# Inputs kept for the last pass: stored as one part and split anew, and two groups to a half of the tokens at a pass's turn

## The chip, the cores and the metric

The kernel runs on 1 core of one Trainium2 chip. The metric is the device time in microseconds: 1502.4 us is the median of 3 runs of the kernel before (1499.89 to 1511.44). One more execution was profiled; it took 1505.07 us.

## The reference

One decoder layer on x (2048 tokens, 1024 channels, float32). The projection is the part that the change touches:

```
hn = rms_norm(x, w_norm)
proj = hn @ w_in                      # 1024 -> 4104 columns
q_a, k_a, v_a, z_a, b_a, a_a, q_b, k_b, v_b, z_b = split(proj)
qkv = silu(causal_conv(q_a, k_a, v_a))        # 4 taps
o_a = gated_delta_rule(l2(q_a), l2(k_a), v_a, g(a_a), sigmoid(b_a))   # 4 heads, in chunks
o_a = rms_norm(o_a) * silu(z_a)
o_b = (softmax(q1 k1) - lam softmax(q2 k2)) v_b                       # 4 heads, causal
o_b = rms_norm(o_b) * silu(z_b)
out = x + concat(o_a, o_b) @ w_out
```

## The kernel before, in words

**Numbers.** Each float32 operand of a large matmul is split into a high part (rounded for the fast matmul format) and a low part (the remainder); a product is three matmuls, high by high, high by low and low by high. So the normalised, transposed input of 512 tokens (an *instance*) is a pair of tiles hh and hl, 128x8x512 each, 2 MB each; the weights of a group of 256 columns are a pair wh and wl, made from wr.

**Passes and groups.** The projection has three passes over halves of 1024 tokens (line 368): the first makes z_a and the six groups of q_a, k_a, v_a for the first half of the tokens (8 groups), the second makes all 16 groups for the second half, the third the attention's columns for the first half (8 groups). Each pass has two instances, so six in all: 0 and 1 in the first pass, 2 and 3 in the second, 4 and 5 in the third. Only two pairs hh, hl and two pairs wh, wl have room. A job is 24 matmuls with 512 moving columns or 48 with 256; a group has 4 jobs or more, half on its pass's first instance and half on its second.

**Inputs.** `x_load` (line 435) loads x in 16 tiles of 128 tokens, into two buffers xt and three buffers x5; `x_scale` normalises a tile (squares on ScalarE, a power on GpSimd, the scaling on VectorE), `x_split` (502) transposes it on TensorE into a PSUM tile tp and splits it: ScalarE copies tp to hh, VectorE subtracts hh from tp into hl. Instances 0 and 1 are needed again in the third pass as 4 and 5. `hx_store` (533) writes their hh and hl to DRAM in quarters while the first pass runs, and `hx_load` (546) reads them into the buffers that instances 2 and 3 leave.

**Weights.** `w_stream` (389) loads one group ahead into two buffers wr (one for each half of the 1024 rows), and splits a group once the group two places before it is through (`w_done`). The load of the next group waits for that split, since it needs wr.

**Order of jobs.** `in_jobs` (562) lists the jobs group by group. The last two groups of a pass are taken together: both on the first instance, then both on the second, so that the first instance is free earlier.

**What sets the order of everything.** The program has streams (generators), each of which yields its next step with an engine and a time. `Flow` (line 31) keeps modelled clocks of the engines and takes the step that could start first (`run`, line 207), and issues it; so the order of each engine's queue is fixed when the program is built, and an engine takes its queue strictly in that order. One changed step moves the ones around it on every engine. TensorE's queue mixes projection jobs with the delta rule's matmuls (tiles psg: a block of `gdn_a` is six matmuls with qk_h and qk_a; fsX makes its decays; then the scan over 16 chunks, with vh, o, S, rr), the transposes tp of x, and in the last third the attention. The loads and most stores go through SyncE's queue (SP).

**Names.** psi: PSUM tile of a projection job. za_s, zb_s, gdx, qk, v: DRAM stages for what the projection made. raw, acc: SBUF tiles of its epilogue. AL: lower triangles of the delta rule.

Of the kernel before, what the change touches and what calls it, by code (L numbers as in the profile page):

```python
# [8 lines left out]
F32 = mybir.dt.float32  # L9
F32R = mybir.dt.float32r  # L10
BF16 = mybir.dt.bfloat16
AF = mybir.ActivationFunctionType
ALU = mybir.AluOpType
# [4 lines left out]
P = 128  # L18
S = 2048
D = 1024  # L20
KT = D // P
# [8 lines left out]
TB = 512  # L30
# [3 lines left out]
class Flow:  # L34
# [119 lines left out]
    def dma(self, out, in_, run=1024, by="SP", **kw):  # L154

        if by == "SP":
            if len(self.dmas) > 7:
                self.free["SP"] = max(self.free["SP"], self.dmas[-8])
            self.op("SP", 475)
        else:  # L160
            self.op(by, 60)
            self.end += 415
        s = max(self.free["DMA"], self.end + 650)
        self.free["DMA"] = s + 4 * math.prod(out.shape) / 250 * (2 if run < 512 else 1)
        (self.nc.sync if by == "SP" else self.nc.scalar).dma_start(out=out, in_=in_, **kw)  # L165
        if by == "SP":
            self.dmas.append(self.free["DMA"] + 1200)
        return self.free["DMA"] + 1200
# [63 lines left out]
def hybrid_kernel(ctx: ExitStack, tc: tile.TileContext, x, w_norm, w_in, conv_w, a_log, dt_bias,  # L232
# [4 lines left out]
    out = out[0]  # L237
# [4 lines left out]
    dram = ctx.enter_context(tc.tile_pool(name="dram", bufs=1, space=DRAM))  # L242

    def r(ap):
        return ap.bitcast(F32R)

    def f(ap):
        return ap.bitcast(F32)
# [9 lines left out]
    zb_s = [dram.tile([P, S], F32, name=f"zb_s{h}") for h in range(H)]  # L258
    o_s = dram.tile([P, 2 * H, S], F32, name="o_s")
    part = dram.tile([S, D], F32, name="part")  # L260
    hx_s = [[dram.tile([P, KT, TB], F32, name=f"hx{i}_{j}") for j in range(2)] for i in range(2)]

    fl = Flow(nc)
    mm, tr, dma = fl.mm, fl.tr, fl.dma
# [118 lines left out]
    HX = {}  # L383
# [51 lines left out]
    def x_load():  # L435
        for n in range(16):

            def best():

                b = x_buf + ([(t_5[0], "ga")] if live5[0] < NX5 else [])  # L440
                return min(b) if b else None

            yield "SP", (lambda: best()[0]), best
            bf = best()
            if bf[1] == "wk":
                x_buf.remove(bf)
                xt = wk.tile([P, D], F32, name="xt", bufs=NXB)
            else:
                live5[0] += 1
                xt = ga.tile([P, D], F32, name="x5", bufs=NX5)  # L450
            n_xl[0] += 1
            t_x = []
            for hs in ([slice(0, TB), slice(TB, D)] if n == 0 else [slice(0, D)]):
                t_x.append(dma(out=xt[:, hs], in_=x[n * P:(n + 1) * P, hs]))
            xq[n] = (xt, t_x[0], bf[1])
            if n == 0:
                for i in range(2):
                    wnb.append(wk.tile([P, TB], F32, name="wnb", tag=f"t1_{i}"))
                    t_wn.append(dma(out=wnb[i], in_=bcast(w_norm)[:, i * TB:(i + 1) * TB]))
                dma(out=ident, in_=c_ident)  # L460
# [72 lines left out]
    def hx_store():  # L533

        for i in range(2):
            yield "SP", (lambda: max(x_ready[i].values())), lambda: all((i, t) in x_done for t in range(4))
            for kh in range(2):
                for j in range(2):
                    yield "SP", NOW, lambda: w_done[0] >= HXW + 3 * (4 * i + 2 * kh + j) // 4
                    t_hx[i] = dma(out=hx_s[i][j][:, kh * 4:kh * 4 + 4], in_=f(HX[i][j][:, kh * 4:kh * 4 + 4]))  # L540

    t_hx = [0.0] * 2
    HXW = 2
# [2 lines left out]
    def hx_load():  # L546
        for i in range(2):
            yield "SP", (lambda: max(t_xu[i + 2], t_hx[i])), lambda: x_used[i + 2]
            hx = (hn.tile([P, KT, TB], F32, name="hh"), hn.tile([P, KT, TB], F32, name="hl"))
            HX[i + 4] = tuple(r(h[:, :, :]) for h in hx)  # L550
            for kh in range(2):
                for j in range(2):
                    yield "SP", NOW, None
                    t = dma(out=hx[j][:, kh * 4:kh * 4 + 4], in_=hx_s[i][j][:, kh * 4:kh * 4 + 4])
                if kh == 0:
                    x_ready[i + 4] = {n: t for n in range(4)}
                x_late[i + 4] = t
            x_done.update((i + 4, n) for n in range(4))

    epi = []  # L560
# [1 line left out]
    def in_jobs():  # L562

        jobs = []
        for gi, (ip, half, kind, arg) in enumerate(groups):
            for tb in range(2):
                if kind == GA and (arg == 0 or gi == 0):
                    js = [[t] for t in range(4)]
                elif kind in (GA, GQ, GV):
                    js = [[2 * t, 2 * t + 1] for t in range(2)]  # L570
                else:
                    js = [c for c in range(2)]
                jobs += [(gi, tb, what) for what in js]
        last = [gi for gi in range(len(groups) - 1) if groups[gi + 1][0] != groups[gi][0]] if SWAP else []
        return sorted(jobs, key=lambda a: (a[0], 0) if a[0] not in last and a[0] + 1 not in last else
                      (a[0] + (a[0] + 1 in last) - 1, a[1]))

    SWAP = True

    def in_proj():  # L580
        KS = 2
# [1169 lines left out]
```

## Time and profile before

| | |
|---|---|
| median of 3 runs | 1502.4 us (1499.89 to 1511.44) |
| the profiled execution | 1505.07 us, span 1503.3 us from the first to the last instruction |
| busy: TensorE (PE), VectorE (DVE), ScalarE (ACT), GpSimd (POOL) | 96%, 63%, 56%, 47% of the span |
| granted TensorE clock, mean | 0.991 |
| DMA | 250.99 MB, mean 167 GB/s |
| projection | until about 998 us; the attention and the output projection run from there to the end |

The profile is one execution. Busy is the time in which an engine executed; an engine that waits for another is idle. PE's matmuls are pipelined, so that a busy PE can still be slower than its best; how far is seen by the number of matmuls in a stretch. A number in brackets at a timeline row is the idle time just before the instruction, with the instruction or transfer that ended it.

### The profile page before, as it was taken

The numbers are of one execution on the slowest core, as the hardware profiler recorded it, in microseconds if no ns is written. First come the engines' busy times: TensorE is split into PE (matmuls) and PEld (weight loads), VectorE is DVE, ScalarE is ACT, GpSimd is POOL, SyncE is SP. The second block draws the span as 40 slices with busy tenths as digits, with TensorE's granted clock in tenths as the row PEclk, the third lists the DMA queues.
The fourth block names the chain that finished last, engine by engine and source line by source line (L and its number), as shares of the span: only waits on it lengthen the run. The fifth ranks groups of instructions, "written<-read, shape, count | busy, mean of one in ns | idle before, by whom it ended". The sixth has DMA issues, their size and how long they took to land.

```text
span 1503.3 us, 28117 instructions
## 1 busy us (share of the span) xinstructions
PE 1447.9 (96%) x9959; PEld 1261.3 (84%) x9959; DVE 954.0 (63%) x2644; ACT 844.4 (56%) x1814; POOL 708.3 (47%) x662
## 2 busy tenths in 40 slices
PE   8899998999998999999999999999999999999998
PEld 6888888988778999998899899877887877888787
DVE  6466887569866667772554453217677777888852
ACT  5354464443565553224536543227777998988870
POOL 3411244600433645554452465625665676776661
PEclk9999999999999999999999999999999999999999
DMA  8665648464745665668766449247666454542425
GB/s 206 163 189 197 173 144 163 122 181 102 169 124 163 171 215 174 152 159 236 241 176 178 132 138 221 86 140 249 217 216 219 141 173 137 190 133 92 134 85 178
DMA packets 282893, 250.99 MB, mean 167 GB/s; under 512 B 47313, under 2 KB 252801, under 8 KB 280705
## 3 DMA queue, kind: packets, MB, share of 16 engines
q1 hardware_dynamic: 257408, 236.61, 55.3%
q10 hardware_dynamic: 25344, 12.59, 2.8%
q8 instruction: 79, 1.29, 0.3%
q14 instruction: 62, 0.50, 0.1%
HBM read 156.86 MB, written 92.27 MB: 166 GB/s over the span
## 4 chain that ended last, share of the span: by engine, by line
PE 74%; DMA 7%; DVE 6%; ACT 5%; POOL 4%; issue 2%; SPq 1%; ACTq 0%; POOLq 0%; DVEq 0%
PE psi L140 36%; PE psb L140 17%; PE pss L140 7%; PE psg L140 7%; PE psb L152 3%; ACT p L81 2%; PE psg L152 2%; PE tp L152 2%; DMA wr<-in_w_in_dram 1%; DMA qk_a<-gdx 1%; SPq L165 1%; POOL t L81 1%; DVE p L81 1%; DMA x<-in_x_dram 1%; DMA za_s<-acc 1%
## 5 line engine op out<-in xcount | busy, mean ns | idle before, releaser
L140 PE MATMUL psi<-wh,hh 128*128 128x256 f32 (+1 forms) x1024 | 305.3, 298 | 8.9 <-ACT acc L81 4.5
L140 PE MATMUL psi<-wl,hh 128*128 128x256 f32 (+1 forms) x1024 | 291.4, 285 | 1.3 <-DVE wl L81 1.3
L140 PE MATMUL psi<-wh,hl 128*128 128x256 f32 (+1 forms) x1024 | 290.9, 284 | 0.0
L81 DVE TENSOR_SCALAR_CACHE_REDUCE p<-pss 128x512 f32<-128x512 f32 (+3 forms) x320 | 179.4, 605 | 69.5 <-PE pss L140 66.6
L140 PE MATMUL psi<-hh,wh 128*128 128x512 f32 x512 | 205.8, 402 | 0.0
L140 PEld LDWEIGHTS psi<-wh,hh 128*128 128x128 f32 x1024 | 197.1, 192 | 10.4 <-ACT acc L81 4.9
L140 PE MATMUL psi<-hh,wl 128*128 128x512 f32 x512 | 202.1, 395 | 0.0
L140 PE MATMUL psi<-hl,wh 128*128 128x512 f32 x512 | 201.3, 393 | 0.0
L140 PEld LDWEIGHTS psi<-wl,hh 128*128 128x128 f32 x1024 | 197.4, 193 | 1.7 <-DVE wl L81 1.5
L140 PEld LDWEIGHTS psi<-wh,hl 128*128 128x128 f32 x1024 | 196.6, 192 | 0.0
L81 POOL TENSOR_TENSOR p<-p,p 128x640 f32<-128x640 f32 (+9 forms) x64 | 162.2, 2538 | 62.9 <-ACT p L81 58.1
L81 ACT ACTIVATE p<-p,nm 128x128 f32<-128x128 f32 (+15 forms) x128 | 153.2, 1200 | 20.8 <-DVE p L81 10.8
L81 ACT ACTIVATE raw<-psi 128x512 f32<-128x512 f32 (+1 forms) x96 | 57.2, 596 | 134.5 <-PE psi L140 113.7
L140 PE MATMUL psb<-th,v 128*128 128x256 f32 (+1 forms) x576 | 126.0, 293 | 1.5 <-DVE tl L81 1.2
L140 PE MATMUL pss<-kk,QQ 64*128 64x512 f32 (+3 forms) x960 | 123.2, 382 | 3.7 <-DVE p L81 1.8
L81 DVE SCALAR_TENSOR_TENSOR acc<-raw,cw,acc 128x512 f32<-128x512 f32 x144 | 112.3, 780 | 14.9 <-ACT acc L81 13.3
L81 ACT ACTIVATE p<-p,sc 128x128 f32<-128x128 f32 (+15 forms) x88 | 108.6, 1253 | 18.6 <-DVE sc L81 16.9
L140 PEld LDWEIGHTS psi<-hh,wl 128*128 128x128 f32 x512 | 96.0, 188 | 22.4
L81 DVE TENSOR_TENSOR tl<-psb,th 128x512 fp32r<-128x512 f32 (+2 forms) x176 | 92.9, 563 | 32.3 <-ACT th L81 30.7
L140 PEld LDWEIGHTS psi<-hl,wh 128*128 128x128 f32 x512 | 96.3, 188 | 20.1
L140 PEld LDWEIGHTS psi<-hh,wh 128*128 128x128 f32 x512 | 96.2, 188 | 19.7
L140 PEld LDWEIGHTS pss<-kk,QQ 64*128 64x128 f32 x960 | 80.3, 184 | 36.7 <-issue 9.3
(212 smaller groups left out, 3311.7 us busy)
## 6 DMA issues: line engine op xcount, KB each, us to landing
wr<-in_w_in_dram SPq DMA_DIRECT2D x80, 256.0 KB
x<-gdx SPq DMA_DIRECT2D x32, 512.0 KB
wr<-in_w_in_dram SPq DMA_DIRECT2D x24, 512.0 KB
gdx<-acc ACTq DMA_DIRECT2D x48, 256.0 KB
kk<-qk SPq DMA_DIRECT2D x48, 256.0 KB
v<-v SPq DMA_DIRECT2D x48, 256.0 KB
qk_a<-gdx SPq DMA_DIRECT2D x32, 256.0 KB
qk<-raw SPq DMA_DIRECT2D x32, 256.0 KB
```

What stands on the lines that cost most here:

```text
L81: return call(*args, **kw)
L140: return self.nc.tensor.matmul(out=out, lhsT=lhsT, rhs=rhs, **kw)
L152: return self.nc.tensor.transpose(out=out, in_=in_, identity=identity)
L165: (self.nc.sync if by == "SP" else self.nc.scalar).dma_start(out=out, in_=in_, **kw)
```

## The change

The two instances that are kept are stored as one part each: GpSimd adds hh and hl, 128x1024 at a time, into a buffer x5, and that is written to DRAM (eight stores of 512 KB in place of eight of 1 MB). To leave a buffer for it, x tiles from the ninth on take at most two of the three x5. For the third pass the sum is loaded into the tile hl, ScalarE copies it, rounded, to hh, and VectorE subtracts hh from it in place; before, both parts were loaded ready. And `in_jobs` takes not only the last two groups of a pass together, but also the first two of the next.

```diff
--- before.py
+++ after.py
@@ -258,7 +258,7 @@
     zb_s = [dram.tile([P, S], F32, name=f"zb_s{h}") for h in range(H)]
     o_s = dram.tile([P, 2 * H, S], F32, name="o_s")
     part = dram.tile([S, D], F32, name="part")
-    hx_s = [[dram.tile([P, KT, TB], F32, name=f"hx{i}_{j}") for j in range(2)] for i in range(2)]
+    hx_s = [dram.tile([P, KT, TB], F32, name=f"hx{i}") for i in range(2)]
 
     fl = Flow(nc)
     mm, tr, dma = fl.mm, fl.tr, fl.dma
@@ -437,7 +437,7 @@
 
             def best():
 
-                b = x_buf + ([(t_5[0], "ga")] if live5[0] < NX5 else [])
+                b = x_buf + ([(t_5[0], "ga")] if live5[0] < NX5 - (n > 7) else [])
                 return min(b) if b else None
 
             yield "SP", (lambda: best()[0]), best
@@ -533,11 +533,17 @@
     def hx_store():
 
         for i in range(2):
-            yield "SP", (lambda: max(x_ready[i].values())), lambda: all((i, t) in x_done for t in range(4))
-            for kh in range(2):
-                for j in range(2):
-                    yield "SP", NOW, lambda: w_done[0] >= HXW + 3 * (4 * i + 2 * kh + j) // 4
-                    t_hx[i] = dma(out=hx_s[i][j][:, kh * 4:kh * 4 + 4], in_=f(HX[i][j][:, kh * 4:kh * 4 + 4]))
+            for k in range(0, KT, 2):
+                yield "POOL", (lambda: max(*x_ready[i].values(), t_5[0])), (
+                    lambda: all((i, t) in x_done for t in range(4)) and live5[0] < NX5
+                    and w_done[0] >= HXW + 3 * (4 * i + k // 2) // 4)
+                live5[0] += 1
+                t = ga.tile([P, 2, TB], F32, name="x5", bufs=NX5)
+                pool.tensor_tensor(out=t, in0=f(HX[i][0][:, k:k + 2]), in1=f(HX[i][1][:, k:k + 2]), op=ALU.add)
+                yield SP
+                t_hx[i] = dma(out=hx_s[i][:, k:k + 2], in_=t)
+                live5[0] -= 1
+                t_5[0] = max(t_5[0], t_hx[i])
 
     t_hx = [0.0] * 2
     HXW = 2
@@ -546,15 +552,23 @@
     def hx_load():
         for i in range(2):
             yield "SP", (lambda: max(t_xu[i + 2], t_hx[i])), lambda: x_used[i + 2]
-            hx = (hn.tile([P, KT, TB], F32, name="hh"), hn.tile([P, KT, TB], F32, name="hl"))
-            HX[i + 4] = tuple(r(h[:, :, :]) for h in hx)
+            hh = hn.tile([P, KT, TB], F32R, name="hh")
+            hx = hn.tile([P, KT, TB], F32, name="hl")
+            t_l = []
             for kh in range(2):
-                for j in range(2):
+                if kh:
                     yield "SP", NOW, None
-                    t = dma(out=hx[j][:, kh * 4:kh * 4 + 4], in_=hx_s[i][j][:, kh * 4:kh * 4 + 4])
+                t_l.append(dma(out=hx[:, kh * 4:kh * 4 + 4], in_=hx_s[i][:, kh * 4:kh * 4 + 4]))
+            for kh in range(2):
+                k4 = slice(kh * 4, kh * 4 + 4)
+                yield "ACT", (lambda: t_l[kh]), None
+                act.activation(hh[:, k4], hx[:, k4], AF.Copy)
+                yield DV
+                dve.tensor_tensor(out=r(hx[:, k4]), in0=hx[:, k4], in1=f(hh[:, k4]), op=ALU.subtract)
                 if kh == 0:
-                    x_ready[i + 4] = {n: t for n in range(4)}
-                x_late[i + 4] = t
+                    x_ready[i + 4] = {n: fl.after("PE") for n in range(4)}
+                x_late[i + 4] = fl.after("PE")
+            HX[i + 4] = hh, r(hx[:, :, :])
             x_done.update((i + 4, n) for n in range(4))
 
     epi = []
@@ -571,11 +585,13 @@
                 else:
                     js = [c for c in range(2)]
                 jobs += [(gi, tb, what) for what in js]
-        last = [gi for gi in range(len(groups) - 1) if groups[gi + 1][0] != groups[gi][0]] if SWAP else []
-        return sorted(jobs, key=lambda a: (a[0], 0) if a[0] not in last and a[0] + 1 not in last else
-                      (a[0] + (a[0] + 1 in last) - 1, a[1]))
-
-    SWAP = True
+
+        new = [gi for gi in range(len(groups)) if gi and groups[gi - 1][0] != groups[gi][0]]
+        two = {}
+        for gi in new:
+            for g in (gi, gi - 2):
+                two[g] = two[g + 1] = g
+        return sorted(jobs, key=lambda a: (two[a[0]], a[1]) if a[0] in two else (a[0], 0))
 
     def in_proj():
         KS = 2
```

What this does to the queues is seen at three places. The first is PE's queue at the start of the second pass, where its first group leaves the pass's first instance (psi: the job's PSUM tile; wh, wl: the group's weights; hh, hl: the instance). Before:

```order
L140 MATMUL psi_2427<-wh_2238,hh_1994 128x256
L140 MATMUL psi_2427<-wl_2239,hh_1994 128x256
L140 MATMUL psi_2427<-wh_2238,hl_1995 128x256
L140 MATMUL psi_2509<-wh_2238,hh_2305 128x256
L140 MATMUL psi_2509<-wl_2239,hh_2305 128x256
L140 MATMUL psi_2509<-wh_2238,hl_2306 128x256
```

Now:

```order
L140 MATMUL psi_2470<-wh_2205,hh_2000 128x256
L140 MATMUL psi_2470<-wl_2206,hh_2000 128x256
L140 MATMUL psi_2470<-wh_2205,hl_2001 128x256
L140 MATMUL psg_2543<-qk_h_2510 128x256
L140 MATMUL psg_2543<-qk_a_2428,qk_h_2510 128x256
L140 MATMUL psg_2543<-qk_h_2510,qk_a_2428 128x256
L140 MATMUL psg_2543<-qk_h_2510 128x256
L140 MATMUL psg_2543<-qk_a_2428,qk_h_2510 128x256
L140 MATMUL psg_2543<-qk_h_2510,qk_a_2428 128x256
L140 MATMUL psi_2556<-wh_2449,hh_2000 128x264
L140 MATMUL psi_2556<-wl_2450,hh_2000 128x264
L140 MATMUL psi_2556<-wh_2449,hl_2001 128x264
```

Before, the same weights went on with the second instance (hh_2305). Now the second group's weights (wh_2449, 264 columns) follow on the same instance (hh_2000), with one block of the delta rule between; the second instance comes after that group's jobs on the first.

The second place is DVE's queue, where the first group's weights of the second pass are split (wl; of its two rows, one for each half of the 1024 rows of w_in). Before:

```order
L81 TENSOR_TENSOR qk_a_2221<-qk_a_2221,qk_h_2274 128x512
L81 TENSOR_TENSOR AL_2253<-psg_2231,ee_2001 128x2x128
L81 TENSOR_TENSOR wl_2239<-wr_1810,wh_2238 128x4x256
L81 TENSOR_TENSOR wl_2239<-wr_1817,wh_2238 128x4x256
L81 TENSOR_TENSOR hl_2306<-tp_2307,hh_2305 128x4x128
```

Now:

```order
L81 TENSOR_SCALAR sn0_2339<-sv0_119 128x2
L81 SCALAR_TENSOR_TENSOR AL_2337<-psg_2310,sn0_2339,ee_2114 128x128 x2
L81 TENSOR_TENSOR qk_a_2342<-qk_a_2342,qk_h_2371 128x512
L81 TENSOR_TENSOR AL_2337<-psg_2310,ee_2114 128x2x128
L81 TENSOR_TENSOR wl_2206<-wr_1810,wh_2205 128x4x256
L81 SCALAR_TENSOR_TENSOR x5_2129<-x5_2129,rsx0_2373,wnb_181 128x512
```

Before, the two wl stood together, ahead of the second instance's first hl. Now the second one (wl_2206 from wr_1810) stands behind a block of the delta rule (sn, AL, qk_a), and ahead of the scaling of an x tile.

The third is ACT's queue in the turn to the third pass, where the loaded sum of instance 4 is split (hh from hl, 128x2048, in two halves). There is no such instruction before:

```order
L81 ACTIVATE o1_8237<-psg_8231,eg1_122 128x128
L81 ACTIVATE hh_8156<-hl_8157 128x2048
L81 ACTIVATE vh0_8131,sso_8230<-og_8229 128x128
L81 ACTIVATE o1_8259<-psg_8234,eg1_122 128x128
L81 ACTIVATE vh2_8261<-psg_8239,sv1_128 128x128
L81 ACTIVATE vh3_8263<-psg_8249,sv1_128 128x128
L81 ACTIVATE acc2_8268<-psi_8171 128x512
L81 ACTIVATE hh_8156<-hl_8157 128x2048
L81 ACTIVATE vh1_8138,sso_8230<-og_8229 128x128
```

The two copies stand among the delta rule's o1 and vh of all heads and the output of one z_b job (acc2).

## Rows read from the trace of the kernel before

**Rows 1.** The page, part 1: busy us, share and instructions of each engine.

```profile
PE 1447.9 (96%) x9959; PEld 1261.3 (84%) x9959; DVE 954.0 (63%) x2644; ACT 844.4 (56%) x1814; POOL 708.3 (47%) x662
```

**Rows 2.** Busy time by stretch; the first row names the columns.

```profile
core 0: us, PE busy (x) PEld busy (x) DVE busy (x) ACT busy (x) POOL busy (x), PEclk, DMA share, GB/s
0.00:75.00 75.00, 61.93 (x429) 56.13 (x430) 42.51 (x69) 35.56 (x86) 28.82 (x45) 0.91 0.74 185
75.00:225.00 150.00, 150.00 (x711) 123.96 (x710) 111.02 (x262) 77.36 (x128) 33.03 (x41) 1.00 0.59 176
225.00:265.00 40.00, 34.19 (x253) 32.55 (x252) 29.03 (x65) 18.57 (x26) 20.44 (x20) 0.91 0.81 153
690.00:750.00 60.00, 58.50 (x437) 50.78 (x435) 24.79 (x64) 28.51 (x107) 26.15 (x37) 1.00 0.79 258
```

**Rows 3.** Timeline of PE, 225 to 262 us: rows with idle time before them.

```profile
237.83 0.38 PE L140 MATMUL psg<-qk_h 128*128 128x256 f32 x1 [1.79 <-ACT qk_h L81]
238.55 0.39 PE L140 MATMUL psg<-qk_a,qk_h 128*128 128x256 f32 x1 [0.34 <-DVE qk_a L81]
...
249.69 0.39 PE L140 MATMUL psg<-qk_a,qk_h 128*128 128x256 f32 x1 [0.96 <-POOL qk_a L81]
...
252.14 0.51 PE L140 MATMUL psg<-fsX,gt 128*128 128x512 f32 x1 [0.50 <-POOL fsX L81]
...
255.58 1.12 PE L152 MATMUL tp<-ident,x 128*128 128x128 f32 x4 [2.07 <-DVE hl L81]
```

**Rows 4.** Busy time in two stretches of the first turn (columns as in rows 2).

```profile
240.00:246.00 6.00, 6.00 (x53) 6.00 (x53) 5.86 (x13) 2.77 (x4) 4.17 (x2) 1.00 0.74 203
255.00:261.00 6.00, 5.42 (x26) 5.42 (x27) 2.51 (x4) 1.23 (x2) 0.96 (x2) 0.50 1.10 314
```

**Rows 5.** Timeline, SP, DVE, ACT, POOL: weights of the second pass's second group.

```profile
230.54 3.92 SPq L165 DMA_DIRECT2D wr<-in_w_in_dram  x2
...
240.45 1.25 DVE L81 TENSOR_TENSOR wl<-wr,wh 128x1056 fp32r<-128x1056 f32 x1
...
242.62 1.08 ACT L81 ACTIVATE wh<-wr 128x1056 fp32r<-128x1056 f32 x1 [1.81 <-DMA wr<-in_w_in_dram]
...
243.78 2.48 POOL L81 TENSOR_TENSOR wl<-wr,wh 128x1056 fp32r<-128x1056 f32 x1 [0.94 <-ACT wh L81]
```

**Rows 6.** Timeline of PE: the first matmul of that pass's first and second group.

```profile
227.16 0.28 PE L140 MATMUL psi<-wh,hh 128*128 128x256 f32 x1
...
265.86 0.28 PE L140 MATMUL psi<-wh,hh 128*128 128x264 f32 x1
```

**Rows 7.** Timeline of DVE: the same scaling of half an x tile, twice.

```profile
239.37 0.74 DVE L81 SCALAR_TENSOR_TENSOR x<-x,rsx,wnb 128x512 f32<-128x512 f32 x1
...
244.03 2.78 DVE L81 SCALAR_TENSOR_TENSOR x<-x,rsx,wnb 128x512 f32<-128x512 f32 x1
```

**Rows 8.** Groups by shape: POOL, ACT, DVE; busy us, mean ns, idle before.

```profile
L81 POOL TENSOR_TENSOR p<-p,p 128x1024 f32<-128x1024 f32 x4 | 9.6, 2398 | 2.1 <-ACT p L81 2.1
...
L81 ACT ACTIVATE p<-p,sc 128x2048 f32<-128x2048 f32 x6 | 12.1, 2014 | 1.0 <-DVE sc L81 1.0
...
L81 DVE TENSOR_TENSOR wl<-wr,wh 128x1024 fp32r<-128x1024 f32 x53 | 69.0, 1301 | 2.8 <-ACT wh L81 1.7
```

**Rows 9.** Issues of the kept inputs (ns min/median/max, starts), and a stretch as rows 2.

```profile
L165 SPq DMA_DIRECT2D hx<-hh x4: 424/458/467, 78.2 to 169.9; - x4
...
L165 SPq DMA_DIRECT2D hh<-hx x4: 319/377/422, 698.5 to 738.0; - x4
L165 SPq DMA_DIRECT2D hl<-hx x4: 425/570/745, 698.9 to 738.4; - x4
...
698.00:708.00 10.00, 10.00 (x81) 8.23 (x80) 5.45 (x17) 4.34 (x15) 3.75 (x7) 1.00 0.98 364
```

**Rows 10.** Timeline of PE, 50 to 75 us: rows with idle time before them.

```profile
60.14 0.39 PE L140 MATMUL psi<-wh,hh 128*128 128x264 f32 x1 [1.11 <-ACT acc L81]
...
70.43 0.39 PE L140 MATMUL psi<-wh,hh 128*128 128x264 f32 x1 [1.32 <-DVE ab L81]
```

## The prediction

> **What bounds the kernel.** I read the busy line of the page first: TensorE (PE) is busy 96% of the span, the next engine 63% [rows 1]. A change that leaves the number of matmuls alone can therefore only give back time in which PE stands idle (some 55 us in all), or runs at half clock. The second view is busy time by stretch [rows 2]: it shows where that idle time lies. From 75 to 225 us PE is busy 150.00 of 150 us: nothing is to be had there. In the first 75 us it is idle for 13.07 us. At the turn from the first to the second pass, 225 to 265 us, it is busy 34.19 of 40 us. At the turn from the second to the third pass, 690 to 750 us, it is busy 58.50 of 60 us; the wait for the reloaded inputs is filled there by the delta-rule work that is mixed in between. The third view is PE's timeline at the first turn: five idle pieces, 1.79 + 0.34 + 0.96 + 0.50 + 2.07 = 5.66 us, with what ended each [rows 3]. The last, 2.07 us at 255.58, is the one that the change speaks of: four transposes of x wait for a buffer that VectorE (DVE) empties with an hl. Just behind it the granted clock is 0.50, its lower level of 1.2 GHz: 26 matmuls in 6 us, where 6 us at 2.4 GHz hold 53 [rows 4]. Some 27 matmuls lost at 6/53 = 0.113 us each are 3.0 us, of which 0.58 are idle time already counted (5.42 of 6 us busy); I take 2.5 us for the clock. So the first turn can give back at most about 8.2 us, which is 0.5% of the kernel.
>
> **The change, part by part.**
>
> *Order at the first turn.* Before, the first group of the second pass needs the second half of its tokens as soon as it is through with the first, at the latest after its 96 matmuls on the first half; they begin at 227.16 [rows 6], and at 53 per 6 us they take 10.9 us. Now 96 matmuls of the second group stand between, another 10.9 us (the order of PE in the section on the change). The transposes that waited at 255.58 are spread over these. I let 0.96 + 2.07 us of idle time (the first ends with a subtraction that POOL made and DVE now makes) and the 2.5 us of half clock go: -5.5. The other 2.63 us I let stay: they wait for a qk_a, which is loaded and split ahead of the delta rule's matmuls, and for an fsX, and both stand in the same places of the new order. What is late next is weights, in two places. (1) The split of the first group's second half of rows now stands on DVE behind the qk_a and the AL of that delta-rule block (order of DVE); PE's next 36 matmuls wait for it. It adds one split, 1.30 us mean [rows 8]. (2) The second group is needed after 96 matmuls and not after 192. Its weights were issued as late as 230.54, and were split by 243.78 + 2.48 = 246.26 [rows 5]; in the old order it began at 265.86 [rows 6], 20 us later. In the new order it is needed at 227.16 + 10.9, plus some 3 us of transposes and delta-rule matmuls between, plus the waits that stay (2.1) and the new one (1.3): 244.5, and its second half of rows 12 matmuls (1.4 us) later, 245.9. That is level with 246.26. Bounds: 0, and 246.26 - 239.4 = 6.9 us if nothing stands between. I take 0.5, near the row. Sum of the first turn: -5.5 + 1.3 + 0.5 = -3.7.
>
> *Start.* From the ninth x tile on, one of three buffers is kept free, so one load of 512 KB goes from the first 60 us to the first turn, and another moves behind a weight load. PE's idle pieces at 60.14 and 70.43, 1.11 and 1.32 us, end with output buffers that wait in the same queue for their store [rows 10]. Bounds 0 and -2.4; I take -1.0. At the turn four tiles instead of three are loaded late; that is inside the 10.9 us of cover above.
>
> *Storing.* Eight stores of 1 MB become eight of 512 KB, and eight additions on GpSimd (POOL) come in: 128x1024 with two inputs costs 2.40 us there [rows 8], 19.2 us in all. POOL is busy 33.03 of 150 us in this stretch [rows 2], so it has room; behind each addition wait za products and delta-rule masks, at most 2.4 us, and PE has projection work. Taken at 0. A DVE instruction that meets a POOL one does pay: the same scaling of half an x tile takes 0.74 us at 239.37 and 2.78 us at 244.03, under a POOL split that lasts until 246.26 [rows 5, 7]. The Trainium skill, page "SBUF — State Buffer", section "Who interferes with whom", has this as a lock: a VectorE instruction with two SBUF inputs and a GpSimd instruction that reads SBUF block each other for a whole instruction. That speaks against moving additions to POOL here; by it DVE would lose up to 19.2 us between 75 and 225. The rows leave it room: DVE is busy 111.02 of 150 us, 39 us are free [rows 2]. So 0 on the path, with 19.2 as the end of the range if that cover is gone.
>
> *Loading and splitting for the third pass.* Before, eight loads of 1 MB land in the two tiles that PE reads [rows 9]. Now four of 1 MB land, and each is copied on ScalarE (ACT; 128x2048 costs 2.01 us) and subtracted on DVE (twice the 1.30 us of 128x1024, an estimate from that row: 2.60) [rows 8]: 8.1 us of ACT and 10.4 us of DVE. The first half of an input is then ready 1 MB earlier and 4.6 us later: at the 364 GB/s of 698 to 708 us [rows 9] 1 MB is 2.9 us, so it is 1.7 us later. PE has no wait for these inputs to lose: it is busy 10 of those 10 us. Idle time to be had is 1.5 us [rows 2]; the ACT copies stand among the delta rule's vh and o (order of ACT), each held up by 2 us. Bounds -1.5 and +18.5; I take 0, because the order keeps projection matmuls between the steps of the delta rule.
>
> *DMA volume.* 8 MB of 251 go. No row shows PE waiting on volume after 75 us except through the qk_a above; 0.
>
> Sum: -3.7 - 1.0 = -4.7 us, from 1505.07 us of the profiled execution (span 1503.3 and 1.8 around it) to 1500.4. That execution lies 2.7 us above the median of the three runs, 1502.4; on the scale of the median it is **1497.7, so 1498 us**.
>
> **Rivals.**
> 1. *Small gain, as summed:* 1498, own range 1493 to 1503. Chance 0.58.
> 2. *All of it comes back.* The first turn gives 5.66 + 2.5, the start 2.4, the second turn 1.5: -12.1, 1490; if delta-rule steps that now run some jobs earlier in the third pass also wait less, 1485. For: nothing in the matmul count resists. Against: 2.63 us of the turn keep their cause, and the weights are as late as before. Chance 0.17.
> 3. *It does not do what it says.* The second group's weights replace x at the turn: 6.9 us of idle time in place of 3.0 and the half clock comes with it, 1502 to 1504. For: they were split at 246.26, level with the need. Against: the order issues them in one go. Chance 0.12.
> 4. *Slower: splits on the scan's path at the second turn.* ACT takes its instructions in order; a copy that waits for its load holds vh and o behind it, and the scan of the delta rule cannot go on. Price: 4 x (2.01 + 2.60) = 18.5 us if each lies on the path, less 4.7: +13.8, 1516. It decides where ACT stands idle before these four copies for more than about 3 us (the 1 MB above) and PE is idle in the same stretch. For: DMA engines are 0.98 busy there [rows 9]. Against: 58.50 of 60 us of PE's time are covered. Chance 0.09.
> 5. *Slower by the lock:* the eight additions land on convolution steps of DVE and the projection runs out of free PSUM banks, +19.2 - 4.7 = +14.5, 1517. For: 2.78 in place of 0.74. Against: 39 us of free DVE time. Chance 0.04. The rule of the skill's page named above would give this time if DVE had no room.
>
> **Range and chances.** A percent, 15 us, is about what a measurement of this kernel can tell from no change; the three runs alone lie 11.6 us apart. From rival 2 I reach down to 1486, from rivals 4 and 5 up to 1514. Faster by over 1% (under 1487) needs the far end of rival 2: 0.11. Slower by over 1% (over 1517) needs all of rival 4 or 5: 0.07. Same: 0.82.
>
> **What would show it.** The order: no PE idle before transposes of x near 255, and clock 1.00 through the turn. The weights: idle before the first 264-column matmul, ended by a wl or wh. The storing: x5 additions of 2.4 us on POOL, and PE still busy 150 of 150 us behind the start. The second turn: ACT's idle time before the 128x2048 copies, and PE's from 690 to 750. The forecast is wrong if PE's total idle time changes by more than 10 us, or if the attention's 500 us move, where I see no cause.

## The result, and the profile after

The changed kernel takes 1528.8 us (median of 4 runs, 1525.8 to 1531.2), the kernel before beside it 1503.5 us (1499.9 to 1511.4): a ratio of 1.0163, 95% interval 1.0142 to 1.0184. The forecast was 1498 us, no change; it is slower by some 25 us, outside the range given.

The page of the kernel after: busy time by engine (answers to [rows 1]), and the chain of work that ended last by engine; then the line with span and mean granted clock.

```profile
PE 1456.9 (95%) x9959; PEld 1265.1 (83%) x9959; DVE 986.5 (65%) x2647; ACT 856.9 (56%) x1822; POOL 736.1 (48%) x669
...
PE 61%; DVE 12%; DMA 11%; ACT 6%; POOL 5%; issue 4%; SPq 2%; ACTq 0%; DVEq 0%; POOLq 0%
```

```profile
core 0: 1525.8 us, clock 0.984
```

The chain of the kernel before, for comparison:

```profile
PE 74%; DMA 7%; DVE 6%; ACT 5%; POOL 4%; issue 2%; SPq 1%; ACTq 0%; POOLq 0%; DVEq 0%
```

Two numbers account for the difference, by an estimate. PE's idle time, span less busy, is 1525.8 - 1456.9 = 68.9 us; before it was 1503.3 - 1447.9 = 55.4: 13.5 more. And a mean clock of 0.984 instead of 0.991 costs about (0.016 x 1525.8) - (0.009 x 1503.3) = 24.4 - 13.5 = 10.9 us of PE time. Together 24.4, with the clock rounded to the third digit, for 22.5 us of span. The number of matmuls has not changed (x9959). So the question is why PE waits more, and where. The chain gives a first hint: DVE's part of it is 12%, where it was 6% before, and PE's 61% instead of 74%.

Busy time by stretch after the change (columns as in [rows 2], of which the first, second, third and last of these rows are the counterparts):

```profile
0.00:75.00 75.00, 61.44 (x435) 56.02 (x436) 41.86 (x68) 33.53 (x81) 27.84 (x43) 0.91 0.69 178
75.00:225.00 150.00, 145.31 (x681) 118.26 (x680) 117.20 (x242) 79.21 (x127) 56.19 (x46) 1.00 0.49 147
225.00:265.00 40.00, 33.07 (x224) 31.01 (x223) 33.79 (x80) 19.38 (x30) 22.08 (x23) 0.91 0.80 157
265.00:690.00 425.00, 399.36 (x2817) 361.37 (x2816) 293.95 (x770) 186.82 (x475) 171.84 (x209) 0.98 0.57 151
690.00:750.00 60.00, 59.30 (x415) 50.30 (x414) 26.20 (x63) 34.66 (x108) 31.35 (x43) 1.00 0.73 181
```

The counterpart of the fourth row, from the kernel before:

```profile
265.00:690.00 425.00, 410.54 (x2908) 372.24 (x2907) 291.87 (x780) 196.73 (x496) 177.77 (x218) 1.00 0.61 157
```

The stretch behind the start, where PE was busy 150.00 of 150 us, now has 4.69 us of idle time and 681 matmuls instead of 711. The first turn gives back nothing: 33.07 us busy instead of 34.19. And 425 us in the middle, of which the forecast said nothing, have 25.64 us of idle time; before it was 14.46. The loss is in the whole projection. It ends at about 1026 us instead of 998; the 500 us behind it are 5 us shorter than before.

PE's timeline from 140 to 270 us, rows with idle time before them (the counterpart of [rows 3]):

```profile
148.44 0.38 PE L140 MATMUL psg<-qk_h 128*128 128x256 f32 x1 [1.05 <-ACT qk_h L81]
150.53 0.38 PE L140 MATMUL psg<-qk_a,qk_h 128*128 128x256 f32 x1 [1.70 <-DVE qk_a L81]
...
233.22 0.39 PE L140 MATMUL psi<-wl,hh 128*128 128x256 f32 x1 [0.97 <-DVE wl L81]
...
240.18 0.39 PE L140 MATMUL psg<-qk_h 128*128 128x256 f32 x1 [4.52 <-ACT qk_h L81]
...
242.00 0.58 PE L140 MATMUL psg<-qk_a,qk_h 128*128 128x256 f32 x1 [1.43 <-DVE qk_a L81]
...
268.95 0.66 PE L152 MATMUL tp<-ident,x 128*128 128x128 f32 x4 [1.15 <-DVE hl L81]
```

The wait before the transposes of x has shrunk from 2.07 to 1.15 us, as the new order was to do. In its stead PE waits 4.52 + 1.43 us for the qk_h and qk_a of a delta-rule block, and part of the turn runs at the lower clock as before (mean 0.91 in both).

What the additions do to DVE is to be seen at 141 to 150 us, in the timeline of POOL and DVE:

```profile
141.88 2.95 POOL L81 TENSOR_TENSOR x<-hh,hl 128x1024 f32<-128x1024 f32 x1
147.57 2.35 POOL L81 TENSOR_TENSOR x<-hh,hl 128x1024 f32<-128x1024 f32 x1 [2.74 <-DMA hx<-x]
...
135.26 2.33 DVE L81 SCALAR_TENSOR_TENSOR acc<-raw,cw,acc 128x512 f32<-128x512 f32 x3 [1.48 <-ACT acc L81]
141.82 4.35 DVE L81 SCALAR_TENSOR_TENSOR acc<-raw,cw,acc 128x512 f32<-128x512 f32 x3 [2.32 <-ACT acc L81]
148.42 2.05 DVE L81 TENSOR_TENSOR qk_a<-qk_a,qk_h 128x512 fp32r<-128x512 f32 x1 [2.26 <-ACT qk_h L81]
```

Three steps of the convolution take 2.33 us without an addition beside them and 4.35 with one. The subtraction that makes qk_a runs until 150.47, the addition beside it until 149.92, and the matmul that needs it starts at 150.53 after 1.70 us of waiting: a POOL instruction has become idle time of PE.

### The profile page after: what moved, and what is told of

It is laid out like the page before. It is cut to its first block, busy times and chain, and to the rows that moved or that the text cites. A ratio compares the mean times of both kernels' runs of the same rounds, so it can differ in the third digit from the quotient of the medians.

```text
span 1525.8 us, 28172 instructions
## 1 busy us (share of the span) xinstructions
PE 1456.9 (95%) x9959; PEld 1265.1 (83%) x9959; DVE 986.5 (65%) x2647; ACT 856.9 (56%) x1822; POOL 736.1 (48%) x669
## 4 chain that ended last, share of the span: by engine, by line
PE 61%; DVE 12%; DMA 11%; ACT 6%; POOL 5%; issue 4%; SPq 2%; ACTq 0%; DVEq 0%; POOLq 0%
PE psi L140 22%; PE psb L140 17%; PE psg L140 7%; PE pss L140 7%; DVE acc L81 4%; PE psb L152 4%; DMA wr<-in_w_out_dram 2%; SPq L165 2%; DMA wr<-in_w_in_dram 2%; PE psg L152 2%; DMA za_s<-acc 1%; ACT acc L81 1%; ACT p L81 1%; POOL rqx L81 1%; DVE wl L81 1%
## 5 line engine op out<-in xcount | busy, mean ns | idle before, releaser
L81 ACT ACTIVATE p<-p,nm 128x128 f32<-128x128 f32 (+15 forms) x128 | 153.2, 1200 | 22.5 <-DVE nm L81 12.3
L81 DVE SCALAR_TENSOR_TENSOR acc<-raw,cw,acc 128x512 f32<-128x512 f32 x144 | 122.0, 847 | 12.8 <-ACT acc L81 11.1
L140 PE MATMUL psb<-woh,oh 128*128 128x512 f32 x256 | 109.6, 428 | 0.0
```

Source lines behind the costliest of these rows:

```text
L81: return call(*args, **kw)
L140: return self.nc.tensor.matmul(out=out, lhsT=lhsT, rhs=rhs, **kw)
```

## The experiments

Two theories stood at the beginning: A, that the POOL additions hold DVE's instructions, and B, that two groups at a time on both sides of a turn come too close together. A third came from the spread of the loss: C, that the program's order is fixed by a model of the engines' clocks, so that any change of it moves steps of the whole program, and some come late. All ratios are to the kernel before, run in turn with it on the same chip, with 95% intervals.

| kernel | order of the kernel's own | another (delay 285) | another (275) |
|---|---|---|---|
| before, nothing changed | 1 | 1.0083 (1.0056 to 1.0111) | 1.0059 (1.0040 to 1.0078) |
| order of jobs alone | 1.0134 (1.0117 to 1.0152) | 1.0059 (1.0038 to 1.0081) | 1.0064 (1.0043 to 1.0085) |
| storage, split, x limit alone | 1.0070 (1.0047 to 1.0092) | 1.0089 (1.0055 to 1.0123) | 1.0227 (1.0196 to 1.0259) |
| the whole change | 1.0163 (1.0142 to 1.0184) | 1.0108 (1.0071 to 1.0146) | 1.0236 (1.0207 to 1.0264) |
| the whole change, additions taken away | 1.0102 (1.0082 to 1.0123) | 1.0073 (1.0048 to 1.0098) | 1.0191 (1.0160 to 1.0223) |

### Nothing of the change, other orders

The planner's delay of a signal to PE is changed from 280 ns to 285, 290 and 275; the program computes the same with the same instructions, in another order.

```
-        return 280 if b == "PE" else 200 if a == "PE" else ...
+        return 285 if b == "PE" else 200 if a == "PE" else ...
```

At 285: 

> The kernel before with nothing of the change: the planner's delay of a signal to PE is 285 instead of 280 ns, which shuffles the order of the steps a little all over the program. Theories A and B: 1500 to 1507 us, since nothing was added. Theory C, that the kernel before has an order that any shuffle spoils: 5 to 25 us slower, with new idle PE of 1 to 6 us in many places of the projection.

At 290: 

> The kernel before with the planner's delay of a signal to PE at 290 instead of 280 ns: a second shuffle of the order, nothing of the change. Theory C, that the order of before is one that nearly any shuffle spoils: 1513 to 1528 us, as the shuffle at 285 (1521). Theories A and B, that the change's own parts cost what was lost and that 285 was one bad draw: 1500 to 1510 us.

At 275: 

> The kernel before with that delay at 275 ns: a shuffle in the other direction. Theory C: 1513 to 1528 us, idle PE and half clock in new places of the projection. Theories A and B: 1500 to 1510 us.

Measured: 1521.4, 1525.2 and 1514.9 us; the ratios are 1.0083, 1.0118 (1.0093 to 1.0142) and 1.0059. Theory C holds: the kernel before loses 0.6 to 1.2% with any of three other orders. From 75 to 225 us PE is as busy as it was. In the order of 285, as [rows 2]:

```profile
75.00:225.00 150.00, 150.00 (x718) 124.75 (x718) 107.17 (x253) 76.55 (x127) 32.36 (x40) 0.99 0.59 176
225.00:265.00 40.00, 34.81 (x241) 32.75 (x241) 30.08 (x68) 17.86 (x26) 19.33 (x17) 0.91 0.82 154
```

The first 75 us have 59.59 us busy there instead of 61.93. The rest is lost behind these stretches, in other places in each order. Two waits of PE at 275:

```profile
487.51 0.77 PE L140 MATMUL psg<-S,x 128*128 128x128 f32 x2 [5.43 <-DVE Ti L81]
...
791.47 0.87 PE L152 MATMUL psg<-ident,x 128*128 128x128 f32 x3 [3.83 <-DMA x<-gdx]
```

and one at 290:

```profile
264.80 0.79 PE L140 MATMUL psg<-fsX,gt 128*128 128x512 f32 x1 [4.73 <-POOL fsX L81]
```

No part of the change is in these kernels.

### The order of jobs alone

```
 def in_jobs():
     ...
+    new = [gi for gi in range(len(groups)) if gi and groups[gi - 1][0] != groups[gi][0]]
+    ...
+    return sorted(jobs, key=lambda a: (two[a[0]], a[1]) if a[0] in two else (a[0], 0))
```

on the kernel before; the storing stays.

In its own order: 

> The kernel before with the new order of jobs alone (two groups on each side of a turn for one half of the tokens, then for the other); the storing and reading back of two parts and the count of x loads stay as before. Theory A, the POOL additions: the order is not what cost, so 1499 to 1504 us, at most the gain of the first turn (-3.7), and at 75 to 225 us the PE rows stay at 150 of 150 busy. Theory B, the order of the pairs: two groups need their weights and their first conv results closer together, at both sides of both turns, so at least 15 of the 25 us appear: 1518 or more. Theory C, any change of the order moves queue positions and some steps come late anywhere: a change of 5 to 15 us at places that the order does not name.

At 285: 

> The order of jobs alone (as the first run of it), with the planner's delay of a signal to PE at 285 ns. If the order of the pairs has a price of its own, 1525 us or more again; if its 1528 was one draw among shuffled orders, 1512 to 1526, the band of the shuffled orders of the kernel before.

At 275: 

> The order of jobs alone, with that delay at 275 ns. Own price: 1525 us or more. One draw: 1512 to 1526, and its idle times in other places than in the first run of it.

Measured: 1528.2, 1517.3 and 1517.4 us. The first alone would have spoken for theory B; the others lie at 1.0059 and 1.0064, in the band of the shuffled kernel before. The mean of the three is 1.0086, that of the three shuffles 1.0087: the order of jobs has no price that these runs can tell. In the first of them the first turn is better:

```profile
225.00:265.00 40.00, 36.69 (x277) 35.14 (x275) 29.45 (x66) 19.95 (x30) 21.09 (x20) 0.96 0.82 155
```

PE is busy 36.69 of 40 us (34.19 before) at a mean clock of 0.96 (0.91): 2.5 us less idle and 0.05 x 40 = 2.0 us less for the clock. The forecast had -3.7 for this turn. The other two orders of it show the like: 35.20 and 35.75 us busy at a clock of 1.00, with 283 and 287 matmuls. In the first order the gain is lost again later, among others here:

```profile
405.04 0.39 PE L140 MATMUL psg<-comp,lr 128*64 128x32 f32 x2 [5.39 <-DMA comp<-d_s]
...
751.77 1.12 PE L152 MATMUL tp<-ident,t 128*128 128x128 f32 x4 [5.99 <-POOL t L81]
```

### The storage alone

The kernel after with the old `in_jobs`:

```
-        new = [gi for gi in range(len(groups)) if gi and groups[gi - 1][0] != groups[gi][0]]
...
+        last = [gi for gi in range(len(groups) - 1) if groups[gi + 1][0] != groups[gi][0]] if SWAP else []
```

In its own order: 

> The kernel after with the old order of jobs: the additions on POOL, one stored part, the split anew and the x limit stay. Theory A, the POOL additions: most of the loss stays, 1518 to 1530 us, and weight casts and conv steps of 2.8 us stand on DVE between 75 and 230 us. Theory B, the order of the pairs: 1500 to 1507 us. Theory C: between the two, with idle PE at other places than in the kernel after.

At 285: 

> The stored sum and the split alone, with that delay at 285 ns. The POOL additions' own price is 5 to 6 us (idle PE of 3 to 5 us between 75 and 230 us): 1518 to 1531, that much above the shuffled orders of before, with PE idle in 140 to 195 us again. If they cost nothing of their own: 1512 to 1526 and no idle PE there.

At 275: 

> The stored sum and the split alone, with that delay at 275 ns. Own price of the additions: 1518 to 1531 with 3 to 5 us of idle PE between 75 and 230 us. Nothing of their own: 1512 to 1526 and none there.

Measured: 1518.0, 1521.4 and 1544.5 us. In each of the three PE is idle between 75 and 230 us (5.2, 3.6 and 5.6 us), as in every kernel with the additions; in none of the six orders of the two groups before is it idle there for more than 0.33. The 1544 is far above the expectation; the kernel with the whole change at the same delay has it too.

### The whole change, in other orders

At 285: 

> The kernel after with that delay at 285 ns: the whole change, in another order. Theory C: 1515 to 1535 us, on either side of the 1528 of after, with the idle times after 250 us in other places than in after (not at 316, 376, 680 and 800 us). Theories A and B, that the change's parts cost 20 us or more wherever the rest stands: 1525 to 1540 us, with the idle times of after in the same places.

At 275: 

> The kernel after with that delay at 275 ns. Theory C: 1515 to 1535 us, and the mean of the three orders of after stands within 8 us of the mean of the shuffled orders of before. Theories A and B: the mean of after's orders stands 15 us or more above the mean of the shuffled orders of before.

Measured: 1524.2 and 1541.9 us. The idle times move in part: at 285 the wait for t at 680 us is gone and one for x from gdx at 314 us stays (3.49 us), at 275 a wait for t stays (5.76 us, at 677) and the one for x at 316 is gone. The mean of the three orders of the change is 1.0169, 0.8% or 12 us above the mean of the shuffled orders of before. The expectation had put C at under 8 and A or B at over 15, so the result lies between them, and with the spread among three orders it does not by itself show that the change has a price of its own. The next two experiments test that with the order kept.

### The additions taken away

The same instructions in the same order on every engine, but each addition becomes a small memset; the planner books the addition as if it were there:

```
-                pool.tensor_tensor(out=t, in0=f(HX[i][0][:, k:k + 2]), in1=f(HX[i][1][:, k:k + 2]), op=ALU.add)
...
+                fl.op("POOL", 150 + 2.1 * 1024)
...
+                nc.gpsimd.memset(t[:, :, :8], 0.0)
...
-                t_hx[i] = dma(out=hx_s[i][:, k:k + 2], in_=t)
+                t_hx[i] = dma(out=hx_s[i][:, k:k + 2], in_=f(HX[i][0][:, k:k + 2]))
```

In the order of after: 

> The kernel after, with the same instructions in the same order on every engine, but each POOL addition of 128x1024 is replaced by a memset of 128x2x8 and the store reads the high part itself (the low part is left out of what is stored, and the transfers stay of the same size). Theory A, the POOL additions hold DVE: the conv steps and casts of 2.8 us between 75 and 230 us go, PE is busy 150 of 150 us there again, and the time falls by 15 to 22 us to 1507 to 1514. Theory B, the order of the pairs, and theory C, the places in the queues: the additions are hidden, so the time stays at 1524 to 1531.

At 285: 

> The kernel after with the delay at 285 ns, same order, each POOL addition replaced by a memset of 128x2x8 and the store reading the high part itself (the low part is left out of what is stored). If the additions hold DVE at a price of about 5 us in every order: 1517 to 1521 (from 1524), and the idle PE at 140 to 230 us falls from 3.5 to under 2 us. If they cost nothing here: 1522 to 1526.

At 275: 

> The same edit on the kernel after with the delay at 275 ns, the slowest order of the change. If the additions are the whole price of the storage: 1520 to 1528 (from 1542). If their price is the 5 us of the other order and the rest is late steps elsewhere: 1535 to 1539.

Measured: 1522.5, 1519.2 and 1539.2 us. Against the table's row above, the ratio falls by 0.0061, 0.0035 and 0.0045, each to about 0.003 to 0.0045, so that the second alone is not clear of nothing. Theory A is right, and covers a fifth to somewhat over a third of the loss in each order; 1522.5 lies between the two expectations for it. PE's idle time from 75 to 225 us falls from 4.69, 3.52 and 5.02 us to 0.88, 0 and 1.41. Up to 230 us it did not fall at 285: 4.15 us are left, all behind 225, in a wait of 5.74 us for wl at the first turn. DVE runs as many instructions as with the additions (x2647 in the order of after) and is 12.4, 12.3 and 9.6 us less busy; and of PE's waits between 75 and 230 us in the kernels with the additions none ends with POOL. So what the traces show is DVE held by the additions, and no wait of PE for POOL itself. The stretch behind the start, and the place of 141 to 150 us, in the order of after (the same work starts 2 to 4 us earlier here):

```profile
75.00:225.00 150.00, 149.12 (x697) 122.07 (x696) 109.33 (x254) 81.19 (x131) 38.18 (x50) 1.00 0.52 151
```

```profile
139.63 2.33 DVE L81 SCALAR_TENSOR_TENSOR acc<-raw,cw,acc 128x512 f32<-128x512 f32 x3 [2.33 <-ACT acc L81]
144.21 0.69 DVE L81 TENSOR_TENSOR qk_a<-qk_a,qk_h 128x512 fp32r<-128x512 f32 x1 [2.26 <-ACT qk_h L81]
```

The convolution steps are back at 2.33 us, the subtraction at 0.69 instead of 2.05, and PE does not wait for it. The late steps at the first turn and behind it stay: PE still waits 6.20 us for t at 673 us, 6.33 in the kernel after.

### The additions put on the kernel before

The test of the same price at the one order that no shuffle has: all instructions of the kernel before stay where they are, and POOL gets the work of the additions, unknown to the planner. They write the norm weight, which the scaling of the x tiles reads; no wait of DVE between 75 and 250 us ends with them.

```
+                    for op in (ALU.add, ALU.subtract):
+                        nc.gpsimd.tensor_tensor(out=wnb[j], in0=wnb[j], in1=f(HX[i][0][:, 2 * kh + j]), op=op)
                     t_hx[i] = dma(out=hx_s[i][j][:, kh * 4:kh * 4 + 4], in_=f(HX[i][j][:, kh * 4:kh * 4 + 4]))
```

> The kernel before with every instruction where it stood, and on POOL, at the eight places of the stores, an addition and a subtraction of 128x512 each (16 instructions, the POOL time of the eight additions of 128x1024; they work on the norm weight, which comes back to its value but for the rounding, and nothing is stored from them). If the additions cost 5 to 9 us whatever the order: ratio to before 1.003 to 1.006, idle PE of 2 to 5 us between 75 and 230 us. If this order has cover for them: 1.000 to 1.002. If this order is one that small delays spoil as a shuffle does: 1.008 or more.

Measured: a ratio of 1.0051 (1.0035 to 1.0066), 7.7 us. It is the price seen in the other orders: 9.2, 5.3 and 6.8 us.

```profile
75.00:225.00 150.00, 146.95 (x695) 119.96 (x694) 112.63 (x243) 74.80 (x124) 52.64 (x53) 1.00 0.58 173
225.00:265.00 40.00, 33.99 (x232) 30.81 (x231) 33.57 (x75) 18.54 (x27) 22.61 (x20) 0.95 0.73 129
```

DVE has 37 us free in the first stretch, and PE is idle for 3.05 us all the same, with 16 matmuls fewer than before.

### The split, the stores, and the planner's price of a store

The split taken away from the kernel after, the order kept; both tiles are loaded from the one stored part:

```
+                nc.sync.dma_start(out=f(hh[:, kh * 4:kh * 4 + 4]), in_=hx_s[i][:, kh * 4:kh * 4 + 4])
...
-                act.activation(hh[:, k4], hx[:, k4], AF.Copy)
-                dve.tensor_tensor(out=r(hx[:, k4]), in0=hx[:, k4], in1=f(hh[:, k4]), op=ALU.subtract)
...
```

> The kernel after with the same order, but without the four copies on ACT and four subtractions on DVE of the second turn: the stored part is loaded into both tiles (a second load of 1024 KB for each copy, values that the split would have parted are left whole). If the split holds the scan on ACT and DVE: 1514 to 1522. If it is hidden, as forecast: 1526 to 1531, or a little more for the loads.

Measured: 1537.3 us, 1.0178 (1.0152 to 1.0204), against 1.0163 with the split. Nothing comes back. The run loads 4 MB more, and two waits of PE for x from gdx are 10.1 us long together instead of 6.9, so the time alone could hide a few us. But in the kernel after, where the copies and subtractions stand between 738 and 793 us, no wait of PE is longer than 0.33 us: the split is not seen on the path.

Half as much stored, on the kernel before; the planner books the whole, and both loads read the part that was stored:

```
-                    t_hx[i] = dma(out=hx_s[i][j][:, kh * 4:kh * 4 + 4], in_=f(HX[i][j][:, kh * 4:kh * 4 + 4]))
...
+                    k = 4 * kh + 2 * j
+                    nc.sync.dma_start(out=hx_s[i][0][:, k:k + 2], in_=f(HX[i][0][:, k:k + 2]))
```

> The kernel before with every instruction where it stood, but each of the eight stores moves half as much, 512 KB (part of one of the two parts; both loads read the one that was stored, so values of the last pass are not the reference's). The forecast took 8 MB less of traffic at 0: ratio 0.998 to 1.002. If the stores hold other transfers: below 0.998.

Measured: 1.0015 (0.9998 to 1.0032). The halved stores give nothing.

One more run asked why steps come late. In the kernel after, the largest wait behind the first turn is that for t at 680.17. Pieces of the chain of waits that leads there (start, us, what), the wait itself in PE's timeline, and two stretches as in [rows 2]:

```profile
642.89 0.61 ACT raw L81
...
648.77 13.15 DMA qk<-raw
662.02 0.61 ACT raw L81
662.65 0.69 DVE acc L81
...
679.08 1.05 POOL t L81
680.17 1.11 PE tp L152 x4
```

```profile
680.17 1.11 PE L152 MATMUL tp<-ident,t 128*128 128x128 f32 x4 [6.33 <-POOL t L81]
```

```profile
640.00:646.00 6.00, 6.00 (x54) 6.00 (x53) 5.02 (x8) 2.15 (x3) 5.25 (x5) 1.00 0.66 226
651.00:657.00 6.00, 6.00 (x54) 6.00 (x53) 5.62 (x14) 0.00 (x0) 0.00 (x0) 1.00 1.01 84
```

A store of 256 KB out of a raw tile took 13.15 us to land, and from 651 to 657 us of that time the DMA engines were busy throughout and moved 84 GB/s. The next epilogue waits for that raw tile, and 18 us later PE waits for what it makes. The planner books every transfer at 250 GB/s. Told 160 GB/s for stores:

```
-        self.free["DMA"] = s + 4 * math.prod(out.shape) / 250 * (2 if run < 512 else 1)
+        self.free["DMA"] = s + 4 * math.prod(out.shape) / (160 if out.space == DRAM else 250) * (2 if run < 512 else 1)
```

> The kernel after with the planner told that a transfer to DRAM moves 160 instead of 250 GB/s, nothing else. If the late steps come from stores that land later than planned (12 us for a store of 256 KB at 650 us): the waits for qk and gdx stores shrink and the time falls to 1505 to 1518. If the late steps have other causes, it is one more shuffle: 1515 to 1542.

Measured: 1538.7 us, 1.0190 (1.0162 to 1.0219). It did not help: this was one more shuffle. That late stores are the common cause is not shown; the wait at 680 is one such case, and the waits of the shuffled orders of before end with Ti, fsX and x from gdx as well.

## Why the prediction was wrong

**What bounds the kernel** was read rightly: PE, and its idle time and clock make up the whole difference.

**The step that failed first is the base of the sum.** "Sum: -3.7 - 1.0 = -4.7 us, from 1505.07 us of the profiled execution" takes it that all that the change does not name stays where it is, although the description of the kernel says that one changed step moves the ones around it on every engine. It moved them: all six orders without the storage part, three with the old order of jobs and three with the new, are 0.6 to 1.3% slower than the kernel before, 13 us in the mean. With the additions taken away, the kernel after is at 1.0102: 15 us of its 25 are not the additions', about what a new order alone costs. How much of the 15 is the order drawn, and how much the steps that storage, split and x limit put into it, was not parted. Both of the prediction's signs of a wrong forecast came: PE's idle time changed by 13.5 us and not by under 10, and the attention's 500 us became 5 us shorter, of which no run gives the cause. But no rival had a moved order as a case, and the range ended at 1514, below the 1516 and 1517 of rivals 4 and 5.

**The term that was mis-sized is the storing**, "Taken at 0" because DVE had 39 us free. It costs 5 to 9 us: 7.7 (5.3 to 9.9) at the order of before, 9.2 in the change's own. Rival 5, with the bound of 19.2 us and a chance of 0.04, had the cause right, additions that hold DVE, but not the way to PE: the projection ran out neither of PSUM banks nor of DVE time, since in the kernels with the additions none of PE's waits between 75 and 230 us stands before a projection matmul. Single steps came 1.4 to 2.1 us later, and PE had the delta rule's blocks that need them (qk_h, qk_a) or transposes next in its queue. So free time of DVE was no cover. The rule of the Trainium skill, page "SBUF — State Buffer", section "Who interferes with whom", which the prediction weighed against the rows and set aside, was right here: the subtraction at 148.42 us, with two inputs in SBUF and 0.69 us long without an addition, ends 0.55 us behind the end of the addition beside it. The runs put the price at about two fifths of the additions' 19.2 us.

**First turn, -3.7.** In the order of jobs alone it gave -4.5 (2.5 us idle, 2.0 clock), so the step was about right in kind and size. In the kernel after it is not there: the transposes wait 1.15 instead of 2.07 us, the split of the weights adds 0.97 (1.3 forecast), and 4.52 us before qk_h and the lower clock take the rest. That wait does not come with the order of jobs. It is 4.52 us also with the storage alone, 4.58 with the additions taken away, and 3.3 in the three kernels with the storage at 275; at 285 all three have 5.7 us in its place that end with wl. The six orders without the storage have no wait of over 2.32 us there, but for the 4.73 at 290. Two rows of ScalarE's queue in the kernel after:

```profile
238.14 0.60 ACT L81 ACTIVATE tp<-x 128x512 f32<-128x512 f32 x1 [0.27 <-DVE hl L81]
...
239.52 0.61 ACT L81 ACTIVATE qk_h<-qk_a 128x512 fp32r<-128x512 f32 x1
```

The squares of the last x tile stand just ahead of that qk_h; in the kernel before the last such squares were done at 216.05. The prediction had these late tiles "inside the 10.9 us of cover". Only part of the 4.52 us can be theirs, and since neither the x limit nor the storing's hold on the x5 buffers was run alone, the cause of this wait is not shown.

**Start, -1.0.** In sum not seen: 61.44 us busy in 75 instead of 61.93, though with 435 matmuls instead of 429. The two pieces that were named did shrink, from 1.11 and 1.32 us to 0.73 and none; others grew.

**Loading and splitting, 0**, and **DMA volume, 0.** Both about right. The copies took 1.9 us on ACT and the subtractions 2.3 to 3.0 on DVE, and without them the time does not fall. Rival 4 did not happen. **Rival 3** did not either: in the kernel after no PE wait of more than 0.97 us at the first turn ends with weights, and the 5.7 us at 285 end with the first group's. **Rival 2** is excluded.

What stays open is why the one order of the kernel before is better than all others tried, what the x limit costs, and why the orders at 275 with the storage, with and without additions, are 1.9 to 2.4% slower. The mean of the three orders with storage but without additions is 1.0122 against 1.0086 of the six others; with a spread of 0.3 to 0.6% among orders that difference is not shown to be a price.

No kernel of the study is faster than the kernel before.

## What to carry to other kernels

Where a program lays out its queues by a modelled clock, a single timing tells of a change and of one draw of an order: run the kernel before and the changed one in three orders each, by a constant that computes nothing, before a difference of a per cent is put down to the change, and put that spread into the forecast. Look for instructions with a short way to TensorE before work is given to another engine that can hold them; a share of free time there says nothing about a step that arrives 2 us late. To price one part, keep every queue as it is and take away or add only that part.

## What the runs showed of the hardware

A POOL addition of 128x1024 with both inputs in SBUF stretches DVE instructions of several kinds that run beside it, and is itself stretched (2.35 to 3.49 us for the eight). A cast with one input, too, at 102 us in the kernel after; without an addition beside it, it takes 0.69 us, and here it ends 0.56 us behind the end of the addition:

```profile
102.10 2.40 POOL L81 TENSOR_TENSOR x<-hh,hl 128x1024 f32<-128x1024 f32 x1
102.23 2.83 DVE L81 CAST wh<-wr 128x1024 fp32r<-128x1024 f32 x1 [0.61 <-PE psi L140]
```

And DMA engines that are busy at a share of 1.01 moved 84 GB/s in 651 to 657 us, with 256 KB stores and, issued just before them, two weight loads of 512 KB under way. The kernel before moved 364 GB/s at 0.98 from 698 to 708 us [rows 9], and the kernel after 226 GB/s at 0.66 from 640 to 646 us; why these transfers were so much slower was not tried.
